# The convolution of an mLSTM stage moved from VectorE to ScalarE and GpSimd, with a weight pool of its own for that stage

## The chip, the cores and the metric

The kernel runs on one core of a Trainium2 chip, as one program. The metric is the device time of one execution in microseconds, as the median of the runs; TensorE (PE), VectorE (DVE), ScalarE (ACT), GpSimd (POOL) and the DMA queue of SyncE (SP) work side by side, each through its own list of instructions in a fixed order, and wait for each other by semaphores.

## The reference

One layer of a decoder block with 512 tokens and a model width of 2048, all in float32. Cut to what matters here:

```python
h = rms_norm(x, norm_g)
q_a, k_a, v_a, o_a, i_a, f_a, z_a, c_q, c_kv, k_r, z_b, g_a, g_b = split(h @ w_in)

qk_a = silu(causal_depthwise_conv(concat([q_a, k_a]), conv_w))   # 4 taps along the tokens, 1024 + 1024 channels
h_a  = mlstm_chunkwise(q_a, k_a, v_a, i_a, f_a)                  # 8 heads, 128 wide for q and k, 256 for v
y_a  = (sigmoid(o_a) * rms_norm(h_a) * silu(z_a)) @ w_a

o_b  = causal_attention(latent q, latent k, v)                   # 16 heads, with rotary parts
y_b  = (o_b * silu(z_b)) @ w_b

out  = x + (sigmoid(g_a) * y_a + sigmoid(g_b) * y_b) @ w_out
```

The convolution of one channel is `out[s] = w[3]*x[s] + w[2]*x[s-1] + w[1]*x[s-2] + w[0]*x[s-3]`, with zeros ahead of the first token.

## The kernel before, in words

**Products.** Every float32 product is made of three matmuls (`mm3`, L112). Each operand is split into a rounded high part and the rest (`split`, L104): ACT casts the high part (L105) and DVE subtracts it from the original (L106). For the weights that is `load_w` (L129): SP loads a tile `raw` of 128 x 512 numbers (L137, 4 buffers), ACT makes `whi` (3 buffers) and DVE `wlo` (2 buffers). Such a tile feeds 12 matmuls.

**Stages.** The program first projects the latents and the values, gates and so on of both branches (with `rx`, `rr`, `wh`, `wl`, to about L700), then runs the attention in eight pairs of heads (`pair_attn`), then the mLSTM stage, then the products with `w_b` (`out_b`), `w_a` and `w_out`. A generator of one stage is woven with a filler of the next one (`weave`): the main one says how much matmul work it wants put in, and the filler gives it. This sets only the order in which the program is written. The order on each engine is decided when the program is built, by a scheduler that goes by dependencies and by when a tile's memory is free, so that an instruction can stand well ahead of its place in the text.

**Memory.** Tiles come from pools; a pool that is closed gives its place to pools opened later, and a tile there waits for the last use of what lay in it. The attention's pools `bpa` and `bpb` are closed after pair 7, and `bph`, the pool of the mLSTM stage's large tiles, is opened; `wp`, the pool of the weights, stays open from before the attention to the end. `g2p` is the pool of reloaded gated values for the product with `w_a`, and `up` holds the four `u` tiles of 1 MB that `out_b` loads (L1119).

**The mLSTM stage.** `pair_qk(0)` projects q and k of heads 0 and 1. Then `heads()` runs the eight heads and is woven with `pair_qk(1)` to `pair_qk(3)` and, in the last two heads, with `out_b(0)`. For one pair, `conv_qk` projects 256 columns of q (32 groups of three matmuls onto two accumulators, the columns' 128 channels on the partitions), and then the same for k. Each accumulator then goes through `evac` of `conv_qk` (L966): POOL sets three columns of `xp` to zero (L969), ACT copies the accumulator behind them (L970), and DVE makes the four taps in one scaled copy (L980) and three fused multiply-adds (L977). ACT takes a tanh (L985), DVE multiplies (L988), ACT casts the high part of the tile `qkT` (L989) and DVE makes the rest (L992). These stand in four closures which `run_later` puts into the projection that follows, one after each weight row. There are 16 such evacuations.

**A head.** `head_load` loads a head's values and gates (`vh`, `vl`, `to`, `og`), DVE multiplies the gates (L1012). `head_mlstm` broadcasts one row (`aux<-nT,pick`, L1017), makes the exponents on ACT (`wda`, `wdb`, L1035), masks on POOL (L1037), multiplies k and q (`aux<-qkT,qkT`, L1039), weighs them on DVE (L1042) and splits the result (`sta`, `stb`), and multiplies with the values (`aux<-vh,sta`). `head_scale` (L1073) and `head_out` (L1079, L1081) of the head before are put between its steps. In `pair_attn` the output of two attention heads is multiplied by its gate on DVE (L856, `go`) and stored by SP (L857, `gb<-go`). The temporaries `xp`, `cv`, `th` and `go` come from one pool of six.

Of the kernel before, what the change touches and what calls it, by code (L numbers as in the profile page):

```python
# [11 lines left out]
F32 = mybir.dt.float32  # L12
F32R = mybir.dt.float32r
BF16 = mybir.dt.bfloat16
I32 = mybir.dt.int32
AF = mybir.ActivationFunctionType
ALU = mybir.AluOpType
AX = mybir.AxisListType

P = 128  # L20
S = 512
T = S // P
# [13 lines left out]

NB_RAW, NB_W, NB_L, NB_A, NB_B, NB_HEAD, NB_T, NB_ACC, NB_AUX = 4, 3, 2, 15, 12, 17, 6, 5, 3
NB_X, NB_RING, NB_HI, NB_LO = 5, 8, 3, 2

KEYS_AHEAD, ATTN_STEP, MLSTM_STEP, OUT_AHEAD, RELOAD_STEP = 8000, 7800, 6000, 10000, 4000  # L40
EARLY = {"lat", "c", "gz", "vh", "vl", "rope", "rk"}
# [3 lines left out]
def hybrid_kernel(  # L45
# [8 lines left out]
    V, A, G, PE, SP = nc.vector, nc.scalar, nc.gpsimd, nc.tensor, nc.sync  # L54
# [11 lines left out]
    def open_pool(name, side="left"):  # L66
        guard = tc.tile_pool(name=name, bufs=1, side=side, reuse_waits="tile")
        pools[name] = (guard, guard.__enter__())
        return pools[name][1]

    def close_pool(name):
        pools.pop(name)[0].__exit__(None, None, None)
# [3 lines left out]
    def nm(s):  # L76
        uid[0] += 1
        return f"{s}_{uid[0]}"

    def const(shape, dt, name):  # L80
        return cst.tile(shape, dt, tag=name, name=name)
# [3 lines left out]
    def big(shape, dt, name):  # L85
        p, n = big_pool[name in EARLY and len(big_pool) > 1]
        return p.tile(shape, dt, tag="big", name=nm(name), bufs=n)

    def tmp(n, name, dt=F32):
        return tp.tile([P, 516], dt, tag="tmp", name=nm(name))[:, :n]  # L90
# [10 lines left out]
    def f32(ap):  # L101
        return ap.bitcast(F32)

    def split(dst_hi, dst_lo, src):  # L104
        A.copy(dst_hi, src)  # L105
        V.tensor_tensor(dst_lo, src, f32(dst_hi), ALU.subtract)  # L106
# [17 lines left out]
        G.tensor_tensor(dst, t, y, ALU.mult)  # L124

    loads = [None]
    wpool = [None]

    def load_w(src, col, width, kn, first=0):  # L129
        per = max(1, 512 // width)  # L130
        hi = lo = None
        for i in range(kn):
            k = (i + first) % kn
            if k % per == 0:
                wp = wpool[0]
                raw = wp.tile([P, per, width], F32, tag="raw", name=nm("raw"), bufs=NB_RAW)
                loads[0] = SP.dma_start(  # L137
                    raw,
                    src[k * P:(k + per) * P, col:col + width].rearrange("(r p) c -> p r c", p=P),
                )  # L140
                hi = wp.tile([P, per, width], F32R, tag="whi", name=nm("whi"), bufs=NB_W)
                lo = wp.tile([P, per, width], F32R, tag="wlo", name=nm("wlo"), bufs=NB_L)
                split(hi, lo, raw)
            yield hi[:, k % per, :], lo[:, k % per, :]

    later = []

    def run_later():
        if later:
            later.pop(0)()  # L150
# [29 lines left out]
    def drain(gen):  # L180
        for _ in gen:
            pass

    def weave(main, filler):
        for want in main:
            while want > 0:
                got = next(filler, None)
                if got is None:
                    break
                want -= got  # L190
# [164 lines left out]
    cw = const([P, KD, 4], F32, "cw")  # L355
# [347 lines left out]
    def load_h(col):  # L703
        return load_w(w_in, col, 256, KD, first=H8)
# [58 lines left out]
    def pair_gate(p, c):  # L763
        gz = c["gz"] = big([P, 2, S], F32, "gz")

        def evac(s, ps):
            th = tmp(512, "th")
            A.activation(th, ps, AF.Tanh, scale=0.5)
            V.scalar_tensor_tensor(gz[:, s, :], th, 1.0, ps, ALU.add, ALU.mult)

        yield from proj_ch(load_h(OFF_ZB + p * 256), 2, get_n, KD, evac)
# [174 lines left out]
    first = pair_gate(0, cs[0])  # L946
# [3 lines left out]
    second = pair_gate(1, cs[1])  # L950
# [7 lines left out]
        cs[p] = None  # L958
    close_pool("bpb")
    close_pool("bpa")  # L960
    big_pool[:] = [(open_pool("bph"), NB_HEAD)]


    def conv_qk(p, base, blk, res):

        def evac(s, ps):  # L966
            k = blk + 2 * p + s
            xp = tmp(516, "xp")
            G.memset(xp[:, 0:3], 0.0)  # L969
            A.copy(xp[:, 3:515], ps)  # L970
            o = big([P, 2, S], F32R, "qkT")
            cv = tmp(512, "cv")
            th = tmp(512, "th")

            def taps(j0, j1):
                for j in range(j0, j1):
                    V.scalar_tensor_tensor(cv, xp[:, j:j + S], cw[:, k, j:j + 1], cv, ALU.mult, ALU.add)  # L977

            def first():
                V.tensor_scalar(cv, xp[:, 3:515], cw[:, k, 3:4], None, ALU.mult)  # L980
                taps(0, 1)

            def second():
                taps(1, 3)
                A.activation(th, cv, AF.Tanh, scale=0.5)  # L985

            def third():
                V.scalar_tensor_tensor(cv, th, 1.0, cv, ALU.add, ALU.mult)  # L988
                A.copy(o[:, 0, :], cv)  # L989

            def fourth():
                V.tensor_tensor(o[:, 1, :], cv, f32(o[:, 0, :]), ALU.subtract)  # L992

            later.extend((first, second, third, fourth))
            res.append(o)

        yield from proj_ch(load_h(base + p * 256), 2, get_n, KD, evac)

    def head_load(h, c):
# [112 lines left out]
            return g[k]  # L1112
        return get

    u_t = []

    def out_b(d):
        u = up.tile([P, T, 512], F32, tag=f"u{d}", name=f"u{d}")
        SP.dma_start(u, gb_g[d])  # L1119
        u_t.append(u)  # L1120

        def evac(t, ps):
            V.scalar_tensor_tensor(u[:, t, :], u[:, t, :], 1.0, ps, ALU.add, ALU.mult)  # L1123

        yield from proj_tok(load_w(w_b, d * 512, 512, KD), 512, get_gb, KD, evac)
# [20 lines left out]
    for want in heads():  # L1146
        if want is not None:
            weave([want], filler)
            continue
        done += 1  # L1150
        if done < 4:
            drain(filler)
            while later:
                run_later()
            if done < 3:
                filler = pair_qk(done + 1)
            else:
                close_pool("htp")
                close_pool("h8p")
                gp = open_pool("gp", "right")  # L1160
                up = open_pool("up", "right")
                gB = []
                get_gb = lazily(gB, reload(gb_d, gp, gB))
                filler = out_b(0)
    drain(filler)
    close_pool("bph")
    g2p = open_pool("g2p")
    for d in range(1, 4):
        drain(out_b(d))

# [13 lines left out]
    for d in range(4):  # L1184
        th = g2p.tile([P, T, 512], F32, tag="gate", name=nm("gate"), bufs=1)
# [15 lines left out]
    for c0, width in ((0, 512), (512, 512), (1024, 512), (1536, 256), (1792, 256)):  # L1201
# [6 lines left out]
            SP.dma_start(out[0, t * P:(t + 1) * P, nb], xo)  # L1208

        drain(proj_tok(load_w(w_out, c0, width, KD), width, get_y, KD, evac_out))  # L1210
    for name in ("g2p", "wp", "up", "gp"):
        close_pool(name)


# [36 lines left out]
```

## Time and profile before

| | before |
| --- | --- |
| median of 3 runs | 2172.4 us (2171.72 to 3008.73) |
| the profiled execution's own time | 2176.62 us |
| its span in the trace | 2174.9 us |
| PE / DVE / ACT / POOL busy | 2121.5 / 1395.4 / 983.0 / 173.2 us |
| mean granted clock of TensorE | 0.991 |

The profiled execution took 4.2 us more than the median. The span is the time from the first to the last instruction in the trace. PE is busy nearly all the time, so the numbers that matter are the few stretches where it waits, and those in which its clock is granted at half (PEclk 0.50 in a window); the other engines' shares say only how close each comes to setting PE's pace.

### The profile page before, as it was taken

What the parts mean: (1) busy time and instruction counts of PE and PEld (TensorE: products, weight loads), DVE (VectorE), ACT (ScalarE), POOL (GpSimd) and SP (SyncE); (2) the same over time, 40 slices, a digit from 0 to 9 for tenths busy, and PEclk for the clock granted to TensorE, in tenths of its full rate; (3) what the DMA queues carried; (4) which work ended last, traced back from release to release, by engine and by line L of the source; (5) the groups of instructions that cost most, each with busy time, mean ns of one, the idle gap of its engine ahead of it and who ended that gap; (6) DMA issues with size and microseconds to landing.
All of it is one profiled execution on the core that took longest, in us unless ns stands there. A gap on an engine that the chain in (4) does not pass through costs nothing. (4 is left out here: it accounts for less than half of the span.)

```text
span 2174.9 us, 28907 instructions
## 1 busy us (share of the span) xinstructions
PE 2121.5 (98%) x10200; PEld 1787.8 (82%) x10200; DVE 1395.4 (64%) x2260; ACT 983.0 (45%) x2025; POOL 173.2 (8%) x306
## 2 busy tenths in 40 slices
PE   8999999999999999899999999999989999999999
PEld 8878888888888888688888888877867888888889
DVE  5877788887778788656666677766565334444333
ACT  7544444444444544445555556454445223222221
POOL 0000000000000000222222222011111000000000
PEclk9999999999999999999999999999999999999999
DMA  6645424633642462632222222464544425332443
GB/s 171 166 166 184 149 90 149 184 108 105 185 149 90 149 204 92 215 89 75 83 77 80 81 80 73 155 190 144 159 134 157 136 97 160 126 131 92 136 131 117
DMA packets 205314, 286.02 MB, mean 132 GB/s; under 512 B 31216, under 2 KB 111472, under 8 KB 204144
## 3 DMA queue, kind: packets, MB, share of 16 engines
q1 hardware_dynamic: 189040, 256.90, 38.9%
q10 hardware_dynamic: 16128, 27.27, 3.6%
q8 instruction: 80, 1.31, 0.3%
q14 instruction: 66, 0.54, 0.1%
HBM read 240.07 MB, written 44.04 MB: 131 GB/s over the span
## 5 line engine op out<-in xcount | busy, mean ns | idle before, releaser
L106 DVE TENSOR_TENSOR wlo<-raw,whi 128x512 fp32r<-128x512 f32 (+3 forms) x432 | 284.3, 661 | 383.5 <-PE acc L114 252.3
L105 ACT CAST whi<-raw 128x512 fp32r<-128x512 f32 (+3 forms) x432 | 259.1, 600 | 526.8 <-PE acc L115 338.0
L106 DVE TENSOR_TENSOR wl<-rx,wh 128x1024 fp32r<-128x1024 f32 x160 | 196.5, 1228 | 114.7 <-PE aux L507 64.7
L105 ACT CAST wh<-rx 128x1024 fp32r<-128x1024 f32 x160 | 168.9, 1055 | 177.9 <-PE acc L508 109.0
L113 PE MATMUL acc<-whi,g 128*128 128x512 f32 x512 | 201.5, 396 | 5.9 <-ACT g L105 5.9
L115 PE MATMUL acc<-whi,g 128*128 128x512 f32 x512 | 199.7, 393 | 1.8 <-DVE g L106 1.8
L114 PE MATMUL acc<-wlo,g 128*128 128x512 f32 x512 | 200.6, 392 | 0.0
L105 ACT CAST wh<-rr 128x1024 fp32r<-128x1024 f32 x120 | 126.4, 1053 | 160.7 <-PE aux L508 88.1
L106 DVE TENSOR_TENSOR wl<-rr,wh 128x1024 fp32r<-128x1024 f32 x120 | 146.3, 1219 | 27.6 <-PE aux L507 14.6
L506 PE MATMUL acc<-wh,sh 128*128 128x512 f32 x400 | 155.6, 389 | 0.0
L507 PE MATMUL acc<-wl,sh 128*128 128x512 f32 x400 | 155.6, 389 | 0.0
L508 PE MATMUL acc<-wh,sl 128*128 128x512 f32 x400 | 155.6, 389 | 0.0
L113 PEld LDWEIGHTS acc<-whi,g 128*128 128x128 f32 x512 | 96.8, 189 | 25.7 <-ACT g L105 6.5
L115 PEld LDWEIGHTS acc<-whi,g 128*128 128x128 f32 x512 | 96.9, 190 | 22.2 <-DVE g L106 2.2
L114 PEld LDWEIGHTS acc<-wlo,g 128*128 128x128 f32 x512 | 96.9, 189 | 20.3 <-DVE wlo L106 0.8
L115 PE MATMUL acc<-h8h,wlo 128*128 128x512 f32 x256 | 102.8, 406 | 10.3 <-DVE wlo L106 10.3
L113 PE MATMUL acc<-whi,y 128*128 128x512 f32 (+1 forms) x320 | 111.1, 348 | 0.0
L115 PE MATMUL acc<-whi,y 128*128 128x512 f32 (+1 forms) x320 | 111.0, 347 | 0.0
L114 PE MATMUL acc<-wlo,y 128*128 128x512 f32 (+1 forms) x320 | 111.0, 347 | 0.0
L113 PE MATMUL acc<-h8h,whi 128*128 128x512 f32 x256 | 103.6, 405 | 2.3 <-ACT whi L105 2.3
L114 PE MATMUL acc<-h8l,whi 128*128 128x512 f32 x256 | 102.5, 400 | 0.0
L113 PE MATMUL acc<-ht,whi 128*128 128x512 f32 x256 | 101.2, 395 | 0.0
(357 smaller groups left out, 5052.6 us busy)
## 6 DMA issues: line engine op xcount, KB each, us to landing
rr<-in_w_in SPq DMA_DIRECT2D x120, 512.0 KB, 4.6
raw<-in_w_in SPq DMA_DIRECT2D x128, 256.0 KB, 2.8
rx<-in_w_in SPq DMA_DIRECT2D x40, 512.0 KB, 5.0
raw<-in_w_b SPq DMA_DIRECT2D x64, 256.0 KB, 3.1
raw<-in_w_a SPq DMA_DIRECT2D x64, 256.0 KB, 3.2
raw<-in_w_out SPq DMA_DIRECT2D x64, 256.0 KB, 3.0
raw<-in_w_ukv SPq DMA_DIRECT2D x32, 256.0 KB, 2.8
raw<-in_w_uq SPq DMA_DIRECT2D x32, 192.0 KB, 2.4
```

The lines of the kernel that those rows point to most:

```text
L105: A.copy(dst_hi, src)
L106: V.tensor_tensor(dst_lo, src, f32(dst_hi), ALU.subtract)
L113: PE.matmul(ps, lh, rh, start=start, stop=False)
L114: PE.matmul(ps, lh, rl, start=False, stop=False)
L115: PE.matmul(ps, ll, rh, start=False, stop=stop)
L506: PE.matmul(out[i], lh[:, tok], hi[:, n, :], start=first, stop=False, skip_group_check=cont)
L507: PE.matmul(out[i], lh[:, tok], lo[:, n, :], start=False, stop=False, skip_group_check=cont)
L508: PE.matmul(out[i], ll[:, tok], hi[:, n, :], start=False, stop=k == H8 - 1, skip_group_check=cont)
```

## The change

**What it does.** In `evac` of `conv_qk`, ACT now reads the accumulator four times, each time scaled by one tap's weight: once into `cv` and three times into a tile `th`. After each of the three, POOL adds `th`, shifted by one, two or three columns, onto `cv` in place. The zero columns, the copy into `xp` and the four DVE instructions of the taps are gone. Tanh, multiplication and split follow as before, as two of three closures (the first one is empty). Per evacuation that is one POOL and one ACT instruction and four DVE instructions less, and four ACT and three POOL instructions more.

The pool `wp` of the weights is closed together with the attention's pools, and `wph` takes its place for the mLSTM stage, with six `whi`, six `wlo` and still four `raw` buffers. At the stage's end `wph` is closed and a `wp` with the old numbers opened. The pool of the `u` tiles is cut in two: `up0` with the first one is opened where `up` was, `up1` with the other three only after `g2p`.

```diff
+NB_W2, NB_L2 = 6, 6
...
-    wpool = [None]
+    wpool = [None, NB_W, NB_L]
...
-                hi = wp.tile([P, per, width], F32R, tag="whi", name=nm("whi"), bufs=NB_W)
-                lo = wp.tile([P, per, width], F32R, tag="wlo", name=nm("wlo"), bufs=NB_L)
+                hi = wp.tile([P, per, width], F32R, tag="whi", name=nm("whi"), bufs=wpool[1])
+                lo = wp.tile([P, per, width], F32R, tag="wlo", name=nm("wlo"), bufs=wpool[2])
...
     close_pool("bpb")
     close_pool("bpa")
+    close_pool("wp")
+    wpool[:] = open_pool("wph"), NB_W2, NB_L2
     big_pool[:] = [(open_pool("bph"), NB_HEAD)]
...
         def evac(s, ps):
             k = blk + 2 * p + s
-            xp = tmp(516, "xp")
-            G.memset(xp[:, 0:3], 0.0)
-            A.copy(xp[:, 3:515], ps)
+            cv = tmp(512, "cv")
+            A.activation(cv, ps, AF.Copy, scale=cw[:, k, 3:4])
+            for d in range(1, 4):
+                th = tmp(512, "th")
+                A.activation(th, ps, AF.Copy, scale=cw[:, k, 3 - d:4 - d])
+                G.tensor_tensor(cv[:, d:], cv[:, d:], th[:, :S - d], ALU.add)
             o = big([P, 2, S], F32R, "qkT")
-            cv = tmp(512, "cv")
-            th = tmp(512, "th")
-
-            def taps(j0, j1):
-                for j in range(j0, j1):
-                    V.scalar_tensor_tensor(cv, xp[:, j:j + S], cw[:, k, j:j + 1], cv, ALU.mult, ALU.add)
-
-            def first():
-                V.tensor_scalar(cv, xp[:, 3:515], cw[:, k, 3:4], None, ALU.mult)
-                taps(0, 1)
-
-            def second():
-                taps(1, 3)
+
+            def silu():
+                th = tmp(512, "th")
                 A.activation(th, cv, AF.Tanh, scale=0.5)
-
-            def third():
                 V.scalar_tensor_tensor(cv, th, 1.0, cv, ALU.add, ALU.mult)
-                A.copy(o[:, 0, :], cv)
-
-            def fourth():
-                V.tensor_tensor(o[:, 1, :], cv, f32(o[:, 0, :]), ALU.subtract)
-
-            later.extend((first, second, third, fourth))
+
+            later.extend((lambda: None, silu, lambda: split(o[:, 0, :], o[:, 1, :], cv)))
             res.append(o)
...
-                up = open_pool("up", "right")
+                ups.append(open_pool("up0", "right"))
...
     close_pool("bph")
+    close_pool("wph")
+    wpool[:] = open_pool("wp"), NB_W, NB_L
     g2p = open_pool("g2p")
+    ups.append(open_pool("up1", "right"))
```

Up to the convolution a line of the changed kernel has a number one higher than before, behind it one about ten lower.

**Where instructions stand now.** The first place is PE at the end of the attention. In a row `out<-in` names the accumulator and what is multiplied; `acc<-h8h,whi` is the q projection of `pair_qk(0)`, and names with `knT`, `krh`, `pta` or `ptb` belong to the attention. Before, PE's list there reads:

```order
L113 MATMUL acc_12593<-h8h_1465,whi_12651 128x512
L114 MATMUL acc_12593<-h8l_1466,whi_12651 128x512
L115 MATMUL acc_12593<-h8h_1465,wlo_12652 128x512
L795 MATMUL aux_12368<-ident,kn_12039 128x128 x4
L113 MATMUL aux_12376<-knT_12332,qnT_12324 128x256
L114 MATMUL aux_12376<-knT_12332,qnT_12324 128x256
L115 MATMUL aux_12376<-knT_12332,qnT_12324 128x256
L810 MATMUL aux_12376<-krh_12346,qst_12345 128x256
L811 MATMUL aux_12376<-krl_12347,qst_12345 128x256
L113 MATMUL acc_12594<-h8h_1465,whi_12651 128x512
```

So the projection is mixed with the attention's last pair. After the change PE's list, from the last scores of pair 7 on, is:

```order
L811 MATMUL aux_12540<-krh_12346,qst_12345 128x512
L812 MATMUL aux_12540<-krl_12347,qst_12345 128x512
L836 MATMUL aux_12555<-ident,pr_12530 128x128 x3
L836 MATMUL aux_12563<-ident,pr_12550 128x128 x4
L114 MATMUL aux_12572<-pta_12512,vh_12040 128x512
...
L115 MATMUL aux_12572<-ptb_12514,vh_12040 128x256
L116 MATMUL aux_12572<-ptb_12514,vl_12041 128x256
L114 MATMUL acc_12597<-h8h_827,whi_12601 128x512
L115 MATMUL acc_12597<-h8l_828,whi_12601 128x512
L116 MATMUL acc_12597<-h8h_827,wlo_12602 128x512
```

The attention's last pair stands alone, and all 96 matmuls of the q projection (the first are the last three rows) come behind its last matmul.

The second place is SP's list at the same point in the program, with the weight loads of `pair_qk(0)` (`raw<-in_w_in`) and the stores of the attention's output. Before:

```order
L857 DMA gb_7332<-go_12316 128x512
L137 DMA raw_12753<-in_w_in 128x2x256
L137 DMA raw_12776<-in_w_in 128x2x256
L137 DMA raw_12797<-in_w_in 128x2x256
L137 DMA raw_12820<-in_w_in 128x2x256
L857 DMA gb_7333<-go_12509 128x512
L137 DMA raw_12841<-in_w_in 128x2x256
L1119 DMA u_14893<-ggb_1580 128x2048
L857 DMA gb_7333<-go_12585 128x512
L137 DMA raw_12859<-in_w_in 128x2x256
```

and after:

```order
L858 DMA gb_7332<-go_12316 128x512
L858 DMA gb_7333<-go_12509 128x512
L1109 DMA u_14945<-ggb_1580 128x2048
L858 DMA gb_7333<-go_12585 128x512
L138 DMA raw_12599<-in_w_in 128x2x256
L138 DMA raw_12617<-in_w_in 128x2x256
L138 DMA raw_12635<-in_w_in 128x2x256
```

`raw_12599` is now the first weight tile of the projection, and it stands behind the store of the attention's last output; before, thirteen of these loads stood ahead of that place. The other three `u` loads now stand among the weight loads of `out_b(1)`.

The third place is PE behind the k projection of pair 3, the last one (`acc<-ht,whi` are its last matmuls), where head 6 begins. Before:

```order
L115 MATMUL acc_14550<-ht_7324,wlo_14793 128x512
L1017 MATMUL aux_14873<-nT,pick 128x512
L113 MATMUL acc_14895<-whi_14901,g_14905 128x512
...
L113 MATMUL acc_14898<-whi_14940,g_14944 128x512
L114 MATMUL acc_14898<-wlo_14941,g_14944 128x512
L113 MATMUL aux_14886<-qkT_14491,qkT_14811 128x512
```

and after:

```order
L116 MATMUL acc_14602<-ht_7324,wlo_14839 128x512
L1007 MATMUL aux_14925<-nT,pick 128x512
L114 MATMUL acc_14947<-whi_14953,g_14957 128x512
L115 MATMUL acc_14947<-wlo_14954,g_14957 128x512
L114 MATMUL aux_14938<-qkT_14539,qkT_14865 128x512
```

Between the last projection matmul and the first product of k and q stood 20 matmuls of `out_b(0)`, and now two. At the same point behind the k projections of pairs 0 to 2 it was 24, 29 and 29, and is 28, 27 and 27. ACT's list behind this last k projection (names `acc_14549`, `acc_14550` before, `acc_14601`, `acc_14602` now) was:

```order
L970 COPY xp_14808<-acc_14549 128x512
L105 CAST whi_14974<-raw_14972 128x512
L970 COPY xp_14814<-acc_14550 128x512
L105 CAST g_14905<-raw_14906 128x512
L105 CAST g_14944<-raw_14945 128x512
L985 ACTIVATE th_14813<-cv_14812 128x512
L105 CAST g_14978<-raw_14979 128x512
L989 CAST qkT_14811<-cv_14812 128x512
```

and is now:

```order
L972 ACTIVATE cv_14854<-acc_14601,cw 128x512
L975 ACTIVATE th_14856<-acc_14601,cw 128x512
L975 ACTIVATE th_14859<-acc_14601,cw 128x512
L975 ACTIVATE th_14862<-acc_14601,cw 128x512
L972 ACTIVATE cv_14866<-acc_14602,cw 128x512
...
L975 ACTIVATE th_14874<-acc_14602,cw 128x512
L981 ACTIVATE th_14895<-cv_14854 128x512
L106 CAST g_14957<-raw_14958 128x512
L981 ACTIVATE th_14900<-cv_14866 128x512
L106 CAST qkT_14865<-cv_14854 128x512
```

Eight scaled copies come first, the cast of `g_14957`, which PE needs for `out_b(0)`, stands behind the first tanh (L981), and the cast of the first channel block's `qkT` behind the second tanh, which needs all six additions on POOL. Behind the k projections of pairs 0 to 2 the two tanh stand ahead of the first cast in the same way.

More of the change, by code (lines that the diff above doesn't have):

```diff
@@ L1113, in lazily @@
         return get
-    u_t = []
+    u_t, ups = [], []
     def out_b(d):
-        u = up.tile([P, T, 512], F32, tag=f"u{d}", name=f"u{d}")
+        u = ups[-1].tile([P, T, 512], F32, tag=f"u{d}", name=f"u{d}")
         SP.dma_start(u, gb_g[d])
@@ L1210, in hybrid_kernel @@
         drain(proj_tok(load_w(w_out, c0, width, KD), width, get_y, KD, evac_out))
-    for name in ("g2p", "wp", "up", "gp"):
+    for name in ("g2p", "wp", "up1", "up0", "gp"):
         close_pool(name)
```

## The prediction, made before the changed kernel ran

> **What bounds the kernel now.** I read the page's first part, then the windows of the stages that the change touches, then what PE waits for in them.
>
> ```profile
> PE 2121.5 (98%) x10200; PEld 1787.8 (82%) x10200; DVE 1395.4 (64%) x2260; ACT 983.0 (45%) x2025; POOL 173.2 (8%) x306
> ```
>
> PE is the bound: 53 us of the span are all that it idles, so no relief of DVE (64%) pays by itself. Only what happens in PE's gaps counts. Two stretches are touched: the end of the attention, in which the q projection of pair 0 lies, and the mLSTM stage. Columns below are the stretch, its length, then busy time and count of PE, PEld, DVE, ACT, POOL, then the granted clock, DMA share and GB/s.
>
> ```profile
> 1337.30:1387.40 50.10, 47.17 (x257) 38.25 (x256) 38.05 (x105) 26.24 (x74) 12.51 (x18) 1.00 0.22 63
> 1387.40:1690.00 302.60, 277.60 (x1311) 227.94 (x1310) 187.69 (x376) 148.25 (x364) 37.14 (x118) 0.95 0.53 166
> ```
>
> In the attention's end PE is idle 2.9 us of 50.1, at full clock. In the mLSTM stage it idles 25.0 us of 302.6, and at a mean clock of 0.95 it loses another 0.05 x 302.6 = 15 us. **40 us** is thus all that any edit can win there, 1.8% of the kernel. PE's waits in that stage name the owners (us in total, times, longest):
>
> ```profile
> PE acc L115 <- DVE wlo L106: 10.1, 6, 2.1
> PE acc L113 <- ACT g L105: 5.9, 2, 4.6
> PE aux L113 <- DVE wda L1042: 2.5, 4, 0.8
> PE acc L113 <- ACT whi L105: 2.3, 1, 2.3
> PE aux L1079 <- DVE og L1073: 1.8, 1, 1.8
> ```
>
> The convolution's DVE work shows here only as late `wlo` tiles, six waits of 1.7 us on average. A gap also costs clock:
>
> ```profile
> 1475.20:1478.60 3.40, 1.95 (x9) 1.29 (x7) 3.38 (x8) 0.62 (x1) 0.09 (x3) 1.00 0.00 0
> 1478.60:1482.00 3.40, 2.73 (x12) 2.27 (x13) 3.40 (x7) 0.94 (x2) 0.00 (x0) 1.00 0.40 90
> ...
> 1543.50:1546.90 3.40, 1.29 (x7) 1.07 (x7) 3.40 (x7) 0.63 (x1) 0.00 (x0) 1.00 0.06 6
> 1546.90:1550.30 3.40, 3.40 (x10) 2.62 (x9) 2.55 (x5) 1.14 (x2) 0.00 (x0) 0.50 0.50 148
> 1628.80:1632.20 3.40, 0.00 (x0) 0.00 (x0) 0.74 (x2) 0.61 (x3) 0.51 (x1) 1.00 1.00 353
> 1632.20:1635.60 3.40, 2.36 (x7) 2.07 (x8) 3.21 (x7) 2.91 (x7) 0.44 (x1) 0.50 0.09 33
> 1635.60:1639.00 3.40, 3.40 (x12) 2.71 (x12) 2.09 (x6) 0.95 (x4) 0.35 (x1) 0.50 0.43 149
> ```
>
> A window in which PE was busy 1.29 of 3.4 us is followed by one at clock 0.50, which loses 1.7 us; an empty one by two, which lose 3.4; after one with 1.95 busy (the first row) the clock stays whole. Where the mean of a gap falls between, I count one half window.
>
> **The change part by part. First, the end of the attention.** The order shows that the projection's 96 matmuls, which lie in the attention's waits now, come behind its last matmul, since their weight loads stand in SP's list behind the last store of the attention (the new pool lies where the attention's tiles lay). The rows that carry this term, of the same window by lines, by the tile `wlo`, and of PE's timeline for the spacing of such matmuls and for the k boundary below:
>
> ```profile
> L113 PE MATMUL acc<-h8h,whi 128*128 128x512 f32 x17 | 7.2, 422 | 0.0
> ...
> L115 PE MATMUL acc<-ht,wlo 128*128 128x512 f32 x16 | 6.2, 390 | 0.0
> ```
> ```profile
> 1337.30:1387.40 50.10, 12.51 (x32) 6.02 (x32) 5.48 (x8) 1.00 0.22 63
> ```
> ```profile
> 1408.89 0.39 PE L115 MATMUL acc<-ht,wlo 128*128 128x512 f32 x1
> ...
> 1409.35 0.39 PE L113 MATMUL acc<-h8h,whi 128*128 128x512 f32 x1
> ...
> 1414.59 0.39 PE L115 MATMUL acc<-h8h,wlo 128*128 128x512 f32 x1
> 1414.88 0.50 PE L113 MATMUL aux<-qkT,qkT 128*128 128x512 f32 x1
> ```
>
> Six groups of 16 or 17 make 97; one starts every (1414.59 - 1409.35) / 23 = 0.228 us, so the 96 take **21.9 us**. The attention alone cannot end sooner than its DVE work allows, 38.05 - 5.48 (eight `wlo`, which leave) = 32.6 us, nor later than the 50.1 us of now. I take 43: 50.1 less the 5.5 us of `wlo` on its busiest engine and about 1.5 us of projection matmuls that stood ahead of an attention matmul. Nearer to the upper end, because the softmax passes between DVE, ACT and PE, and what leaves PE there was filling waits. Then comes the start of the projection:
>
> ```profile
> 1385.62 0.28 PE L115 MATMUL aux<-ptb,vl 128*128 128x256 f32 x1
> ...
> 1385.94 0.69 DVE L856 TENSOR_TENSOR go<-aux,gz 128x512 f32<-128x512 f32 x1 [1.24 <-PE aux L115]
> ...
> 1386.65 0.34 SPq L857 DMA_DIRECT2D gb<-go  x1
> ```
> ```profile
> u<-ggb SPq DMA_DIRECT2D x4, 1024.0 KB, 6.6
> raw<-in_w_in SPq DMA_DIRECT2D x6, 256.0 KB, 4.6
> ```
> ```profile
> raw<-in_w_in SPq DMA_DIRECT2D x128, 256.0 KB, 2.8
> ```
>
> From the last attention matmul to the store's issue it is 1.1 us with its 0.34; a weight load lands 2.8 us after issue (median of the page), or 4.6 beside a `u` load (the DMA answer for 1380 to 1400), and a cast takes 0.6: 4.5 to 8 us, I take **6**. The gap brings an empty window: 3.4 us; the bare attention, 47.2 - 21.9 = 25 us of matmuls in 43, lies between the rows' 0.38 and 0.57 busy, so a window or so falls: another 1.6 (0 to 6). Sum: 43 + 6 + 21.9 - 50.1 + 5 = **+26 us**, between 33 + 4.5 + 22 - 50 + 2 = +11 and 50 + 8 + 22 - 50 + 10 = +40.
>
> **Second, the convolution.** Prices by line (min/median/max):
>
> ```profile
> L977 DVE SCALAR_TENSOR_TENSOR cv<-xp,cw,cv x48: 740/744/830, 1388.5 to 1618.2; 128x512 f32<-128x512 f32 x48
> L980 DVE TENSOR_SCALAR cv<-xp,cw x16: 474/480/490, 1387.5 to 1614.0; 128x512 f32<-128x512 f32 x16
> L985 ACT ACTIVATE th<-cv x16: 629/633/640, 1390.8 to 1619.0; 128x512 f32<-128x512 f32 x16
> L989 ACT CAST qkT<-cv x16: 613/619/624, 1392.4 to 1620.8; 128x512 fp32r<-128x512 f32 x16
> L1081 ACT ACTIVATE go<-aux,mgh x16: 667/682/691, 1458.3 to 1685.6; 128x512 f32<-128x512 f32 x16
> L757 POOL TENSOR_TENSOR qro<-qro,qrt x8: 1264/1289/1627, 937.1 to 1344.0; 128x512 f32<-128x512 f32 x8
> ```
>
> DVE loses 16 x (0.48 + 3 x 0.744) = 43.4 us. ACT gains 64 copies at 0.68 (L1081, also a scaled copy from PSUM) less 16 plain ones, some 34 us, and has 154 us free. POOL, the price that matters, gets 48 additions; the nearest row is an addition in place of the same size (L757): 48 x 1.29 = 62 us. All of this is beside PE, except where PE waits for `qkT`: behind each of the four k projections. Now the chain from the last projection matmul to the first `aux<-qkT,qkT` took 6.0 us (1408.89 to 1414.88) and 24 fill matmuls covered it without a gap. The new one: two scaled copies until the second addition's operand is there (1.4), six additions for both blocks (7.7), the second tanh (0.63), since the first block's cast stands behind it in ACT's list, and the cast (0.62): 10.4 us. The cover is 28, 27 and 27 matmuls, 6.3 us, so PE waits 4.1 us; at the fourth boundary it is two matmuls and the broadcast, 0.7 us, and the wait 9.7. Sum 22 us; another us at each for POOL and DVE holding each other up (next row) makes **26**. The ends: at DVE's price of 0.74 an addition, 9 us; at the largest L757, 1.627, with that us, 34. Clock: three gaps with one half window, one with two: **8.5 us**.
>
> ```profile
> 1348.02 1.90 POOL L760 TENSOR_TENSOR kn<-kn,rs 128x1024 f32<-128x1024 f32 x1
> ...
> 1348.26 1.67 DVE L817 TENSOR_TENSOR nmx<-nmx,srq 128x1 f32<-128x1 f32 x1
> ```
>
> This DVE instruction on one column took 1.67 us and ended with POOL's.
>
> **Third, six buffers and a freer DVE.** In the changed lists the splits of heads 2 to 5 stand three to four tiles further ahead. I let the waits for `wlo`, `whi` and `g` go (10.1 + 2.3 + 5.9) with their half windows; what is late next is `wda` (2.5) and a few late `whi`, since only four `raw` buffers feed the six: **8 us** stay with clock (4 to 15). At the stage's end, the chain through `og` now has 12 matmuls ahead of the transposes and not 25: the 1.8 us wait becomes 1.8 + 13 x 0.228 = 4.8, and a half window: **6.5** (3 to 8). The three `u` loads that move among the weights of `out_b` I cost at nothing: four loaded `raw` tiles, 4 x 12 x 0.228 = 11 us of matmuls, hide the 6.6 us of one; without that cover it is up to 6 us once.
>
> The stage then loses 26 + 8.5 + 8 + 6.5 = 49 us where it lost 40: **+9** (from -20 to +25).
>
> **Sum:** +26 + 9 = +35 us; the profiled 2176.6 becomes 2212. That execution was 4.2 us over the median of the runs shown, so the forecast is 2172.4 + 35 = **2207 us**, +1.6%.
>
> **A rule on the clock.** The windows above show half clock after gaps of about 2 us. The Trainium skill, TensorE: Matmul & The Clock Gate, section "Why this matters for your kernels", asks only for no PE-idle gaps over about 3 us. By that, the bare attention and the stage's 2 us gaps would cost no clock, and the time would be some 5 us lower, 2202, inside the forecast's own case. The trace differs (1.29 us busy in the window from 1543.50, then 0.50), so I go by the rows.
>
> **The rivals.**
> *The stage wins.* If the additions lie in the fill (9 us in all, as at DVE's price) and the six buffers take all late splits, the stage loses 20 and not 40 us; with the tail at +26 that is 2172.4 + 6 = 2178, and with a cheap tail 2163. For it: 115 us of free DVE time, 265 of POOL. Against: L757 at 1.29, and the order itself, which gives the last boundary two matmuls of fill.
> *Slower than before by over 2%.* POOL and DVE lock each other. The mechanism: an addition that runs while DVE has `wlo` or `og` to subtract or multiply holds it until it ends, as in the row of 1348.26, so at each boundary six additions at 1.63 hold the splits of the fill, too. The waits there are then 34 us, their half windows 12, the late splits 15, the end 8: 69 for 40, +29; with +26 of the tail 2172.4 + 55 = 2227. It decides once the additions' mean is over 1.5 us. The Trainium skill, GPSIMD Engine Reference, section "8. Key points", says that GpSimd shares its SBUF interfaces with VectorE and contends with instructions that have two SBUF inputs. The row agrees in kind; what 48 additions do, no row shows.
> *The tail is free.* If the scheduler's order mattered little because the attention's end runs near its DVE limit (33 us), the tail costs +11, and the sum is 2172.4 + 20 = 2192. Against it: DVE idles 12 of 50 us now, in a chain.
>
> **How the numbers follow.** Forecast (2190 to 2225, which takes in the free tail): 0.52. The stage wins (2160 to 2190): 0.22. Locked (2225 to 2250): 0.20. Left over on either side: 0.03 each. The range holds the forecast and most of the two others, 2176 to 2240. A measurement tells 2% from no change, 2129 to 2216: faster 0.02; slower takes the locked case, its remainder and the upper quarter of the forecast, 0.37; within, 0.61.
>
> **What would show it.** Right: no `acc<-h8h` matmul before the attention's last; a PE gap of 4.5 to 8 us there with clock 0.50 behind it; the stretch from the attention's last pair to the end of the q projection at 71 to 77 us for 50; four waits for `qkT`, the last twice the others; fewer waits for `wlo`; L976 near 1.3 us. Wrong: a bare attention of 35 or of 50 us; additions below 0.9 or above 1.6 us; waits for `whi` in place of `wlo`, because four `raw` buffers or the DMA set the pace.

## The result: 2.5% slower

The changed kernel took 2227.1 us (2225.35 to 2230.68) against 2172.4: a ratio of 1.0249 (1.0226 to 1.0272), some 54 us more. One execution of the kernel before, of 3008.73 us, was a slow one and is left out of both numbers. The profiled executions differ by 2223.7 - 2174.9 = 48.8 us of span (that of before was 4.2 us above its median), and the readings below account for those. The first part of the page, after:

```profile
PE 2133.2 (96%) x10200; PEld 1800.7 (81%) x10200; DVE 1387.1 (62%) x2196; ACT 1011.7 (45%) x2073; POOL 227.7 (10%) x338
```

POOL gained 54.5 us. DVE lost 8.3 us, though the instructions taken from it were worth 43: most came back as longer ones (see below).

The clearest cut is by PE's own landmarks. (1) the last matmul of the attention's inputs to the last one of the attention; (2) from there to the first `aux<-qkT,qkT`; (3) the first to the last `aux<-qkT,qkT`, that is the eight heads; (4) from there to PE's last matmul.

| us | (1) attention's end | (2) to first qkT | (3) heads | (4) rest |
| --- | --- | --- | --- | --- |
| before | 50.0 | 29.3 | 244.6 | 511.5 |
| after | 52.7 | 62.2 | 254.3 | 516.3 |
| difference | +2.7 | +32.9 | +9.7 | +4.8 |

These add up to 50.1; the stages ahead were 1.8 us faster, and what follows PE's last matmul took 0.3 us more.

**The attention's end.** Windows of the changed kernel, columns as before; the first is the attention's end and the second the gap behind it:

```profile
1335.50:1386.80 51.30, 33.06 (x161) 26.16 (x159) 32.81 (x96) 21.47 (x64) 12.39 (x17) 0.84 0.05 17
1386.80:1393.00 6.20, 0.19 (x2) 0.03 (x1) 0.74 (x2) 0.62 (x1) 0.00 (x0) 0.78 0.92 333
```

The stretch is no shorter than before, though 96 matmuls and all of the projection's splits have left it, and PE's mean clock is 0.84. In the gap PE stands while the DMAs run at 333 GB/s. The timeline shows the chain that the prediction added up:

```profile
1386.55 0.41 PE L116 MATMUL aux<-ptb,vl 128*128 128x256 f32 x1
1387.00 0.69 DVE L857 TENSOR_TENSOR go<-aux,gz 128x512 f32<-128x512 f32 x1 [3.09 <-PE aux L116]
1387.72 0.32 SPq L858 DMA_DIRECT2D gb<-go  x1
1388.08 2.15 SPq L138 DMA_DIRECT2D raw<-in_w_in  x4
1392.30 0.62 ACT L106 CAST whi<-raw 128x512 fp32r<-128x512 f32 x1 [8.85 <-DMA raw<-in_w_in]
...
1392.97 0.79 PE L114 MATMUL acc<-h8h,whi 128*128 128x512 f32 x1 [6.01 <-ACT whi L106]
```

Store, load, cast, matmul: 6.4 us between the two starts. The last row's matmul takes 0.79 us, where 0.39 to 0.50 are usual at full clock: the granted clock is 0.50 there.

**The mLSTM stage.** PE's waits from 1387 us on:

```profile
PE aux L114 <- ACT qkT L106: 14.7, 4, 4.2
PE aux L114 <- DVE wda L1032: 14.3, 4, 3.9
PE acc L114 <- ACT g L106: 6.1, 1, 6.1
PE acc L114 <- ACT whi L106: 6.0, 1, 6.0
PE aux L1069 <- DVE og L1063: 4.4, 1, 4.4
```

All waits for `wlo` are gone. There are four for `qkT`, one at each k boundary, and four for `wda`, which before the change had cost 2.5 us in all. The latter fall in heads 1, 3 and 5 (11.3 us in all) and 7 (3.0 us); the timeline of head 1:

```profile
1479.06 1.03 POOL L121 TENSOR_TENSOR rs_y<-msn,mhalf 128x4 f32<-128x4 f32 x1 [0.63 <-DVE msn L1054]
...
1480.33 1.08 POOL L976 TENSOR_TENSOR cv<-cv,th 128x509 f32<-128x509 f32 x1
...
1481.52 0.28 POOL L1027 TENSOR_SCALAR_AFFINE_SELECT wda<-wda 128x128 f32<-128x128 f32 x1
...
1482.57 0.48 DVE L1063 SCALAR_TENSOR_TENSOR og<-num,rsn,og 128x256 f32<-128x256 f32 x1 [3.59 <-POOL rsn L1057]
1482.97 0.68 DVE L1032 SCALAR_TENSOR_TENSOR wda<-aux,wda 128x512 f32<-128x512 f32 x1
...
1483.71 0.58 PE L114 MATMUL aux<-qkT,qkT 128*128 128x256 f32 x1 [3.44 <-DVE wda L1032]
```

POOL's list has the head's mask (L1027) and the end of the reciprocal root (`rsn`) behind an addition of the next pair's convolution, and DVE's list has `og`, which waits for that `rsn`, ahead of `wda`, which PE needs. In head 7 no addition is left, as the last one ends at 1658 us; there `og` waits for the reciprocal root without one, and stands ahead of `wda` again:

```profile
1696.41 0.48 DVE L1063 SCALAR_TENSOR_TENSOR og<-num,rsn,og 128x256 f32<-128x256 f32 x1 [2.31 <-POOL rsn L1057]
...
1698.90 0.68 DVE L1032 SCALAR_TENSOR_TENSOR wda<-aux,wda 128x512 f32<-128x512 f32 x1
...
1699.63 0.39 PE L114 MATMUL aux<-qkT,qkT 128*128 128x256 f32 x1 [3.00 <-DVE wda L1032]
```

**What became of DVE's 43 us.** One line of DVE that the change doesn't touch, before, and after:

```profile
L1073 DVE SCALAR_TENSOR_TENSOR og<-num,rsn,og x32: 469/477/485, 1452.4 to 1684.2; 128x256 f32<-128x256 f32 x32
```
```profile
L1063 DVE SCALAR_TENSOR_TENSOR og<-num,rsn,og x32: 475/1303/1512, 1482.6 to 1727.6; 128x256 f32<-128x256 f32 x32
L976 POOL TENSOR_TENSOR cv<-cv,th x48: 1079/1272/1949, 1418.0 to 1656.6; 128x511 f32<-128x511 f32 x16, 128x510 f32<-128x510 f32 x16, 128x509 f32<-128x509 f32 x16
```

The median of this multiplication went from 0.477 us to 1.303. The 20 of the 32 that met one of POOL's additions took 1.25 to 1.51 us, the other 12 0.48 to 0.51; in all that is 18 us more. The timeline (rows with x2 or x4 are runs of instructions, with their sum) shows them in step:

```profile
1512.60 5.31 POOL L976 TENSOR_TENSOR cv<-cv,th 128x509 f32<-128x509 f32 x4
1512.72 2.74 DVE L1063 SCALAR_TENSOR_TENSOR og<-num,rsn,og 128x256 f32<-128x256 f32 x2
...
1515.38 1.57 DVE L982 SCALAR_TENSOR_TENSOR cv<-th,cv 128x512 f32<-128x512 f32 x1
1516.88 1.57 DVE L107 TENSOR_TENSOR wlo<-raw,whi 128x512 fp32r<-128x512 f32 x1
```

Four additions in 5.31 us, and beside them no DVE instruction of two SBUF inputs takes less than 1.3 us, where 0.48 and 0.68 are usual. That agrees with the Trainium skill, GPSIMD Engine Reference, section "8. Key points", which names contention with DVE instructions that have two SBUF inputs; the price is this trace's. The additions grow too, but less: one that met no DVE instruction takes 1.08 us (1.29 on 511 columns), these four 1.15 to 1.47.

### The profile page after: what moved, and what is told of

Same layout as the page of the kernel before. It is cut to its first block, busy times and chain, and to the rows that moved or that the text cites. A ratio compares the mean times of both kernels' runs of the same rounds, so it can differ in the third digit from the quotient of the medians.

```text
span 2223.7 us, 28894 instructions
## 1 busy us (share of the span) xinstructions
PE 2133.2 (96%) x10200; PEld 1800.7 (81%) x10200; DVE 1387.1 (62%) x2196; ACT 1011.7 (45%) x2073; POOL 227.7 (10%) x338
## 6 DMA issues: line engine op xcount, KB each, us to landing
rr<-in_w_in SPq DMA_DIRECT2D x120, 512.0 KB, 4.7
rx<-in_w_in SPq DMA_DIRECT2D x40, 512.0 KB, 4.9
```

## The experiments

The theory after the result: the weight pool's new place costs the attention's end, POOL's additions cost the stage, and the six buffers win something. Its rival: the convolution is the whole loss, and the attention's end would have been slow anyway. Ratios are to the kernel before on the same chip, with 95% intervals; the columns are the four stretches of the profiled execution. The kernel before took 2173.5 and 2173.7 us beside E1 to E9, and 2175.9 and 2176.3 us beside E10 to E13. Between these two groups the ratios and the stretches compare, and not the medians.

| run | median us | ratio | (1) | (2) | (3) | (4) |
| --- | --- | --- | --- | --- | --- | --- |
| E1 convolution alone | 2198.8 | 1.0112 (1.0096 to 1.0128) | 50.0 | 38.1 | 256.2 | 510.8 |
| E2 pools alone | 2195.3 | 1.0101 (1.0086 to 1.0116) | 53.1 | 58.3 | 229.5 | 515.5 |
| E3 pools, same size | 2180.3 | 1.0030 (1.0018 to 1.0041) | 49.4 | 29.5 | 245.2 | 516.9 |
| E4 E1, additions on DVE | 2179.1 | 1.0022 (1.0012 to 1.0033) | 50.0 | 31.2 | 243.5 | 511.8 |
| E7 pools, one buffer more | 2211.4 | one run | 52.2 | 58.3 | 242.3 | 516.1 |
| E12 E2, spare matmuls | 2187.7 | 1.0059 (1.0036 to 1.0083) | 47.4 | 56.7 | 222.4 | 515.9 |
| E6 old convolution, extra buffers | 2159.0 | 0.9936 (0.9922 to 0.9950) | 50.0 | 30.3 | 226.9 | 511.3 |
| E9 E6, new convolution | 2193.4 | 1.0099 (1.0080 to 1.0118) | 50.0 | 38.1 | 250.8 | 512.5 |
| E8 E9, additions on DVE | 2174.0 | 1.0000 (0.9990 to 1.0009) | 50.0 | 31.2 | 238.2 | 513.0 |
| E10 E6, three more copies | 2159.3 | 0.9936 (0.9911 to 0.9960) | 49.9 | 30.9 | 225.5 | 511.2 |
| E11 E6, first tap on ACT | 2164.6 | 0.9948 (0.9932 to 0.9965) | 50.0 | 29.8 | 230.1 | 512.0 |
| E13 E8, in steps | 2162.8 | 0.9934 (0.9921 to 0.9948) | 50.0 | 30.8 | 227.1 | 511.7 |

**E1, the convolution alone.**

```diff
 # the changed kernel
-    close_pool("wp")
-    wpool[:] = open_pool("wph"), NB_W2, NB_L2
...
-    close_pool("wph")
-    wpool[:] = open_pool("wp"), NB_W, NB_L
+ # and one pool "up" for the four u tiles, as before
```

> The new convolution with the old weight pool (three whi, two wlo, one pool up). In PE's order the q projection is mixed with the attention's last pair again, as before the change. Theory (the pool's new place costs the attention's end, the convolution costs the stage): the attention's end takes about 50 us again and the 6.3 us gap behind it is gone, so some 31 us of the 53 come back: about 2196 us, 1.010 of before, with waits of PE for qkT (about 15 us in all) and for wda (about 14) still there, and waits for wlo back in part. Rival (the convolution on POOL and ACT is the whole loss, and the bare attention would have been slow in any case): above 2215 us.

The attention's end is 50.0 us again, and some 30 of the 54 us are back. The new convolution alone costs 25 us; the profiled execution shows +8.8 us in (2), +11.6 in (3) and no loss in (1) and (4). The waits that showed as `wda` and `qkT` are in part waits for `wlo` here (20.0 us, 6 times), since two buffers hold less of what DVE is late with: in E9 below, with six, those come to 2.5 us.

**E2, the pools alone.** The changed kernel with `evac` of `conv_qk` as it was.

> The old convolution on DVE with the new pools (six whi, six wlo, pool opened after the attention's pools are closed). The order of the attention's end is that of the changed kernel: no projection matmul in it. Theory: the end of the attention loses 31 us as in the changed kernel; in the mLSTM stage the waits for wlo (10 us and the half clock behind them, 18 together) go, since two buffers were the reason for them: about 2174 + 31 - 14 = 2191 us. Rival (late wlo tiles came from DVE's taps, and more buffers don't help while DVE makes the taps): waits for wlo stay at some 10 us, 2205 us.

Both halves of the theory show: stretches (1) and (2) cost 32 us, and the heads take 229.5 us, 15 less than before, without a wait for `wlo`. E1's and E2's losses, 25 and 22 us, add up to 47 of the 54, but not stretch by stretch: in the heads +11.6 and -15.1 would give -3.5, and the changed kernel has +9.7.

**E3 and E7, what about the pool costs.**

```diff
 # E2; E3 has the old numbers, E7 one wlo more
-NB_W2, NB_L2 = 6, 6
+NB_W2, NB_L2 = 3, 2
```

> As the run with the pools alone, but the reopened pool has the old numbers (three whi, two wlo). PE's order at the attention's end is the old one. Theory (what matters is that the larger pool doesn't fit in the old place and lies over the attention's tiles): the time of before, 2174 us within 0.3%, the attention's end at 50 us. Rival (closing and opening a pool there is what delays the loads, whatever its size): 2174 + 31 = 2205 us.

> The old convolution with the reopened pool, which has three whi and three wlo: one wlo buffer more than before. Theory (a pool that is larger by any amount doesn't fit in the old place and goes over the attention's tiles, so the whole loss comes with the first buffer): attention's end 53 us without projection matmuls, gap of 6 us behind it, 2174 + 31 + 5 and a few us less from wlo waits: 2200 to 2210 us. Rival (the loss grows with the size, since only the tiles that lie over the attention's wait): within 8 us of the same-size run, under 2188 us.

With the old size the attention's end is as before; with one buffer of 2 KB a partition more it is all lost at once (52.2 and 58.3 us; one execution, but 32 us more than E3 in these two stretches). So it is the place, not the number, as far as these runs can tell; the addresses themselves no trace shows. E3's 0.3% is in stretch (4), +5.4 us: with `wp` closed and reopened at the stage's end, whatever its size, PE's list has 12 and not 25 matmuls ahead of the last head's transposes, and PE waits 4.3 us for `og` and not 1.8, with 3.4 us of half clock behind it. The expectation had missed that.

**E12, the attention's end at full clock.**

```diff
 # E2
+    spare = acc()
+    for _ in range(96):
+        PE.matmul(spare, get_n(0)[0][:, :P], get_n(0)[0], start=True, stop=True)
     close_pool("bpb")
     close_pool("bpa")
```

> The run with the pools alone, and 96 more matmuls of 128x512 between the attention and the mLSTM stage whose result nothing reads; in PE's order 77 of them lie in the waits of the attention's last pairs and 19 in the gap behind them. PE thus has the work of the fill, but DVE and ACT don't have its splits. Theory (the bare attention is a chain whose length PE's other work doesn't change, and it was slow because of PE's half clock there, 16 us of the window): the attention's end takes 45 to 50 us at full clock in place of 53, the gap behind it stays near 6 us, and the time falls by 4 to 10 us, 2185 to 2191 us, although PE does 22 us more work. Rival (the chain is as long at full clock): 53 us, 2193 us or more. The prediction's own value, 43 us, would give 2183.

The windows of the attention's end, E2 and E12:

```profile
1336.40:1389.50 53.10, 35.20 (x172) 27.98 (x172) 34.55 (x101) 23.21 (x73) 12.60 (x19) 0.82 0.04 16
```
```profile
1336.70:1384.10 47.40, 44.15 (x248) 35.87 (x247) 34.59 (x101) 23.16 (x73) 12.60 (x19) 1.00 0.05 17
```

PE has 76 matmuls more, DVE and ACT the same work, and the stretch is 5.7 us shorter, at a clock of 1.00 and not 0.82. Work that nobody needs made the kernel some 8 us faster (7.7 by the medians, 9 by the ratios). The three profiled executions with a bare attention, the changed kernel, E2 and E7, took 52.2 to 53.1 us there, at a clock of 0.82 to 0.85. So the clock is most of what lies between 47 and 53 us. How long the bare chain is at full clock no run shows to the end, since some spare matmuls may stand ahead of the attention's own. The heads of E12's profiled execution were 7.1 us shorter than E2's, too, at a clock of 0.99 and not 0.97; that has no cause in the edit that a run shows, and the two profiled executions are 13.8 us apart, more than the medians.

**E4, the additions on VectorE.**

```diff
 # E1
-                G.tensor_tensor(cv[:, d:], cv[:, d:], th[:, :S - d], ALU.add)
+                V.tensor_tensor(cv[:, d:], cv[:, d:], th[:, :S - d], ALU.add)
```

> The new convolution with the old weight pool, and its three additions on VectorE and not on GpSimd. Theory (the additions' price on POOL, 1.27 us, and POOL's queue ahead of the head's masks and the reciprocal root make the waits for qkT and wda): the chain behind a k projection falls from 10.4 to about 7 us, the waits for qkT to 6 us in all (the last boundary), those for wda to under 5: about 15 us below the run with the convolution alone, 2181 us. Rival (ACT's eight copies in a row and the cast behind the second tanh make the waits): within 5 us of the run with the convolution alone, 2191 to 2196 us.

20 us back, more than the 15 expected, and `og` takes its old time:

```profile
L1061 DVE SCALAR_TENSOR_TENSOR og<-num,rsn,og x32: 476/480/486, 1448.5 to 1684.7; 128x256 f32<-128x256 f32 x32
```

**E6, the buffers without the place.** `wp` stays as it is; behind `pair_qk(0)` a second pool adds three `whi` and four `wlo`, used by turns.

```diff
 # the kernel before (u tiles in two pools as in the change)
+                ex, slot = wextra
+                wextra[1] = (slot + 1) % (NB_W + NB_WX)
+                ph, nh = (ex, NB_WX) if ex and slot >= NB_W else (wp, NB_W)
+                pl, nl = (ex, NB_LX) if ex and slot >= NB_L else (wp, NB_L)
...
     drain(pair_qk(0))
+    wextra[:] = open_pool("wx"), 0
...
+    wextra[0] = None
+    close_pool("wx")
     close_pool("bph")
```

> The old convolution and the old pool wp, which stays open; behind pair_qk(0) a further pool with three whi and four wlo is opened (six of each by turns), and closed at the stage's end; the u tiles are cut in two pools as in the change. The first tiles of the q projection are thus in the old place, and PE's order mixes it with the attention's end. Theory (the buffers are worth the 15 us of lost time that the stage had less with them, and the place costs the rest): attention's end 50 us, the stage's loss about 31 us and not 46, 2173.5 - 15 = 2159 us, up to 5 us more if the cut of u costs at the stage's end as with the reopened pool: ratio 0.993 to 0.996. Rival (the stage's gain came only because the stage started later, with more weights loaded ahead): 2170 us or more, ratio over 0.998.

2159.0 us, as the theory had it: **faster than both kernels**, by 0.64% than the one before. Nothing of the gain came from a later start of the stage.

**E9 and E8, the new convolution on top.** E6 with the changed kernel's `evac` (E9), and with its additions on VectorE (E8).

> The changed kernel's convolution (additions on GpSimd) with the extra buffers in place of the reopened pool: what is left of the change when the place of the pool is mended. Theory (additive parts): the changed kernel's 2227 less the attention's end (22 + 6 us and its clock, 31) and the stage's end (5): 2191 us, ratio 1.008; og on DVE at about 1.3 us as in the changed kernel, against 0.48 before. Rival (the extra buffers make up for POOL's hold on DVE): within 0.3% of before, 2167 to 2180 us.

> As the run with the extra buffers, with the new convolution whose three additions are on VectorE. Theory: DVE has 10 us less to do than with the old taps, but the fourth boundary has 3 matmuls of fill and not 23, so a wait of some 6 us for qkT or g comes back: 2162 us. Rival (fewer DVE instructions are worth their own time in wlo waits): 2150 us.

E9 says what the change would have been with its pool in a harmless place: still 1% slower. In the heads the new convolution costs 24 us with six buffers (E6 to E9) and 12 with the old ones (before to E1). Its `og` takes 1.305 us, and the waits of 14 us for `wda` and 13 for `qkT` are there. E8 missed: the additions on VectorE win 19 us, but it stays 15 above E6, not 3.

**E10 and E11, is it ACT's load?**

```diff
 # E10: E6, with
             A.copy(xp[:, 3:515], ps)
+            for d in range(3):
+                A.activation(junk, ps, AF.Copy, scale=cw[:, k, 2 - d:3 - d])
 # E11: E6, with the first tap as
+            A.activation(cv, ps, AF.Copy, scale=cw[:, k, 3:4])
-                V.tensor_scalar(cv, xp[:, 3:515], cw[:, k, 3:4], None, ALU.mult)
```

> The run with the old convolution and the extra buffers, and in each evacuation three more scaled copies of the accumulator on ACT, whose result nothing reads: ACT's load of the new convolution without its additions. Theory (the new convolution with DVE additions lost its 15 us because ACT's copies stand ahead of the casts of weights, g and qkT that PE waits for): half or more of that comes back as loss, 2167 to 2174 us, with waits of PE for whi, g or wda. Rival (the loss is the order of its steps, two tanh ahead of the first cast and 3 matmuls of fill at the last boundary, or DVE's additions): within 4 us of 2159 us.

> The run with the old convolution and the extra buffers, with only the first tap (the scaled copy, 0.48 us on DVE) moved to one scaled copy on ACT. Theory (with six buffers no wait for wlo is left for DVE's relief to win, and ACT's queue is what matters): no gain, 2157 to 2165 us. Rival (DVE's 8 us are worth something at the boundaries): 2152 us or less.

E10 refuted my theory: with 48 more copies on ACT the ratio is E6's, 0.9936, where the theory had asked for 8 us more at least. In ACT's order at the k boundaries casts stand between these copies behind the first four or five; E8 has all eight in a row. E11 is within its range, and its 0.9948 can't be told from E6's 0.9936, as the intervals overlap: 8 us of relief of DVE by itself won nothing.

**E13, the order of the steps.**

```diff
 # E8: the three taps go into the closures
-            for d in range(1, 4):
-                th = tmp(512, "th")
-                A.activation(th, ps, AF.Copy, scale=cw[:, k, 3 - d:4 - d])
-                V.tensor_tensor(cv[:, d:], cv[:, d:], th[:, :S - d], ALU.add)
+            def tap(d):
+                th = tmp(512, "th")
+                A.activation(th, ps, AF.Copy, scale=cw[:, k, 3 - d:4 - d])
+                V.tensor_tensor(cv[:, d:], cv[:, d:], th[:, :S - d], ALU.add)
...
-            later.extend((lambda: None, silu, lambda: split(o[:, 0, :], o[:, 1, :], cv)))
+            later.extend((lambda: tap(1), second, third, fourth))
```

> The run with the additions on VectorE and the extra buffers, but its scaled copies and additions put into the four steps between the projection's rows, as the old taps were, and not all at the accumulator's end. In ACT's list block 1's cast now stands ahead of block 2's tanh, two casts of g ahead of both, and the last boundary has 15 matmuls of fill and not 3. Theory (the 15 us between that run and the one with the old convolution come from the order of the steps, since ACT's copies alone cost nothing): most of them come back, 2159 to 2166 us. Rival (they come from the longer way by ACT and DVE in turn for each tap, in whatever order): 2170 us or more.

The second to fourth step hold the other taps and the tanh, the multiplication and the cast, and the rest. Nearly all of the 15 us are back: the ratio is 0.9934, E6's 0.9936, and stretches (2) to (4) are 12.8 us shorter than E8's and 1.1 longer than E6's. PE's waits of E8 and of E13:

```profile
PE aux L114 <- DVE wda L1035: 7.5, 9, 1.7
PE acc L114 <- ACT g L106: 6.3, 1, 6.3
PE aux L114 <- ACT qkT L106: 4.9, 2, 2.5
PE acc L114 <- ACT whi L106: 3.4, 1, 3.4
```
```profile
PE aux L114 <- DVE wda L1047: 6.0, 5, 2.6
PE aux L114 <- ACT qkT L994: 3.9, 2, 2.0
PE acc L114 <- ACT g L106: 2.8, 1, 2.8
```

The wait for `g` at the last boundary, which sat behind the first tanh, is 2.8 us for 6.3, and that for `whi` is gone. Which of the moved steps does it, the copies, the additions or the tanh, was not separated.

## Why the prediction was right, and where it was off

It said 2207 us in a range of 2176 to 2240, and the time was 2227: inside the range and the way forecast, but above the forecast's own 2190 to 2225. It is the price that the prediction had put on its slower rival, at a chance of 0.20. That the two numbers meet is in part luck, as the rival's terms did not come as told: it had 26 us at the attention's end, 34 us of waits at the k boundaries and additions of over 1.5 us, and the runs showed 32, 21 and 1.28 us (mean), and 14.3 us of waits for `wda`, for which the forecast had kept 2.5. Where the prediction has +26 and +9, the profiled executions show +32 at the attention's end and the projection, and +18.5 in the stage: 4 at its first k boundary, 9.7 in the heads and 4.8 at its end.

**The attention's end and the projection: +26 forecast.** Stretches (1) and (2) gave +35.6, of which about 4 belong to the first k boundary, which the forecast counts with the convolution (62.2 us in stretch (2), and 58.3 in E2 with the old one): +32. The mechanism was as told: no projection matmul ahead of the attention's last, then a gap. The gap was forecast at 6 and measured at 6.4 us. The term that failed is **the bare attention, taken as 43 us, and 44.6 with its clock**: by the window that the prediction measured in it took 51.3 (1335.50 to 1386.80, shown above; 52.7 by the landmarks), on the far side of the 50 us that it had named as a sign of being wrong. The sign of being right failed with it: from that window's start to the end of the q projection it was 82 us, and not 71 to 77. This is the projection's last matmul:

```profile
1416.87 0.39 PE L116 MATMUL acc<-ht,wlo 128*128 128x512 f32 x1
```

E12 shows 47.4 us at full clock (by the landmarks, where the kernel before has 50.0), with spare matmuls in the waits. Of the 7 us that the forecast took off for the `wlo` and the matmuls that leave the stretch, 2.6 came off there; that the rest had lain in the chain's own waits is likely, and no run shows it. The second miss is the clock, 1.6 us forecast: 5.7 measured, the difference of E2 and E12. The forecast had put the bare attention between its two rows of 0.38 and 0.57 busy; its own 25 us in 43 are 0.59, above both, and the mean hid the single windows. Windows of the changed kernel:

```profile
1346.60:1350.00 3.40, 0.96 (x7) 0.73 (x7) 2.50 (x5) 1.46 (x4) 2.44 (x3) 1.00 0.00 0
1350.00:1353.40 3.40, 2.94 (x10) 2.31 (x9) 1.14 (x3) 0.79 (x3) 0.00 (x0) 0.50 0.00 0
1356.80:1360.20 3.40, 1.76 (x12) 1.27 (x12) 3.27 (x5) 2.79 (x5) 1.45 (x4) 1.00 0.00 1
1360.20:1363.60 3.40, 1.73 (x9) 1.43 (x7) 2.29 (x9) 0.89 (x4) 0.27 (x2) 0.51 0.00 0
...
1377.30:1380.70 3.40, 1.29 (x7) 0.60 (x5) 2.60 (x10) 1.96 (x5) 0.00 (x0) 1.00 0.19 72
1380.70:1384.10 3.40, 2.54 (x8) 1.89 (x9) 1.73 (x5) 1.05 (x4) 0.00 (x0) 0.50 0.00 0
```

A window with 1.29 of 3.4 us busy was followed by half clock again, as in the prediction's rows, and so was one with 1.76. PE's longest gaps in these two were 1.74 and 1.56 us. The rule of gaps over about 3 us in the Trainium skill, TensorE: Matmul & The Clock Gate, section "Why this matters for your kernels", again asks for too little.

**The convolution: 26 us of waits forecast.** Those for `qkT` came to 14.7 us, 2.9 to 4.2 each, where 4.1 had been forecast for three and 9.7 for the last; there PE stood 6.1 us for `g` first, whose cast waits behind the same tanh, so that the chain was as long as forecast under two names. An addition took 1.27 us (1.29 forecast). The forecast had kept 2.5 us for `wda`; they came to 14.3, in heads 1, 3, 5 and 7. It had looked at the k boundaries only; the q evacuations of the next pair fall into heads 1, 3 and 5, and their additions stand in POOL's list among the head's own steps. Head 7 has none, and why the lists' order is worse there than before is not shown. Together, 35 us of waits where 26 and these 2.5 had been forecast. E9 against E8 puts 19 us on POOL's additions, and E8 against E13 another 13 on the order of the steps, here with the additions on DVE. How much of the wait in the odd heads is POOL's list and how much DVE's longer instructions was not separated.

**POOL and DVE: one us a boundary forecast.** The rival had an addition hold DVE's instruction until it ends, and the additions grow to 1.63 us. The first came: `og` grew by 0.83 us in the median. The second did not, at a median of 1.27. So the mechanism was the rival's, but the additions' mean, by which it was to be known, did not show it.

**The six buffers: the waits for `wlo`, `whi` and `g` go.** Those for `wlo` did, and E2's and E6's heads are 15 and 18 us shorter than before. In the changed kernel the new convolution took more than that back. One wait for `whi` of 6.0 us is the gap behind the attention.

**The stage's end: 6.5 us forecast with its half window.** PE waited 4.4 us for `og` and not 1.8, and stretch (4) was 4.8 us longer. The `u` loads cost nothing that a wait shows.

## What to carry to other kernels

When a pool is reopened larger, look in the built order at what its first tiles wait for: 2 KB more moved some 22 us of matmuls out of a place where they were free, and the fix was to leave the old pool and add a second one later. Work moved from VectorE to GpSimd is not off VectorE if both read two SBUF operands at that time. And a step's place among the casts that PE waits for can be worth more than its duration: 48 more copies on ACT among the casts were free (E10), and the same convolution cost some 13 us more with its steps in one block than spread over four (E8 and E13).

## What the runs showed of the hardware

A DVE instruction with two SBUF inputs that meets a GpSimd addition mostly takes 1.25 to 1.57 us in place of 0.48 to 0.69; the addition itself goes from 1.08 us to 1.15 to 1.42 (on 509 and 510 columns; 1.95 twice, beside an instruction of 1024 columns). Four DVE instructions that read an accumulator (`wda` and `wdb`, L1022) and met an addition kept their 0.34 us. And matmuls that nobody needs can pay: 96 of them, some 22 us of PE's time, made E12 some 8 us faster than E2, with the attention's end at a clock of 1.00 and not 0.82.
